# Attention scores of a two-layer decoder trunk with 128-row operands in place of 64-row ones

## The chip, the cores and the metric

The kernel runs on one core of a Trainium2 chip. The metric is the device time of one execution in microseconds. TensorE (PE) does the matrix products and transposes; it has two streams, the loads of the stationary operand (PEld) and the products (PE). VectorE (DVE), ScalarE (ACT) and GpSimd (POOL) do the rest, and SyncE (SP) issues the transfers.

## What is computed

The reference is a trunk of two layers over 256 tokens of width 1024. Each layer is a half-step SwiGLU, a token mixer and a second half-step SwiGLU, each with its own norm, shift, scale and gate. The mixer of layer 0 is forgetting attention, that of layer 1 a dilated window attention with three groups of keys per head. Both have 16 heads of width 64:

```python
# layer 0, per head and block of 128 queries (kv_len = 128 or 256)
logits = einsum("bhqd,bhkd->bhqk", q, k[:, :, :kv_len]) * hd ** -0.5
logits = logits + cum[:, :, q0:kv_len, None] - cum[:, :, None, :kv_len]
p = softmax(where(causal, logits, -inf));  o = p @ v
# layer 1, per head, block of queries and each of 3 (window, dilation) groups
logits = einsum("bqhd,bqkhd->bhqk", qb, kb) * hd ** -0.5
```

In layer 0 the term of the query alone cancels in the softmax, so the kernel adds the key's term only (the bias product below). In layer 1 the three groups share one softmax, since they are merged by their denominators.

## The kernel before

All large products have float32 accuracy out of float32r operands: a weight unit of 512 KiB is loaded by SP (`raw`), split by ACT into a high part `wh` (line 206) and by DVE into a low part `wl` (line 215), and used in three products, high by high, low by high and high by low. The class `Weights` keeps up to five units split ahead of their use. PE's order is written by hand: `tick()` passes once per half unit of weights, and work queued with `at(delay, fn)` is issued after so many ticks, between the weight products. The orders on DVE, ACT and POOL come from a scheduler.

The two mixers go through the heads in four groups of four (`HG`), and for each group:

- `in_proj` makes q and k of the four heads for both token tiles (two banks of [128 tokens, 256 of q | 256 of k]). `head_norm` (line 852) takes the norm of each head: ACT squares, DVE sums, POOL takes the root (lines 858 and 860), DVE scales into `qn`.
- `head_transpose` (line 872) turns `qn` on PE (line 878) into a bank [64 x 2 heads, pair, token]. DVE copies the q half with its gain into `qT` (line 880), ACT the k half into `kT` (line 881). In both, the even head of a pair lies on partitions 0 to 63 and the odd head on 64 to 127.
- For group 0 of the dilated mixer `head_stack` (line 883) does the same in float32r parts: `qs` has a head's high part on its own 64 rows and its low part on the other 64, `ks` the high part of k twice, `kl` the low part of k on the head's own rows.
- `attention` (line 902) runs eight steps per group of heads, one per head and token tile. `scores` puts the logits of a step into a bank; DVE adds the mask and takes the row extremum (line 916), ACT the exponential (line 918). Two or three ticks later `turn` transposes the result on PE (line 928) and ACT copies it to `pt` (line 930). `values` multiplies it with v for two heads at once, in different columns of the array (line 941). `close` and `normalize` divide by the sums.

A step of layer 0 (line 1094 and 1095) is a bias product with all 128 rows over 256 columns, in float32r, and one float32 product of `qT` and `kT` on the head's 64 rows, over 128 columns for token tile 0 and 256 for tile 1. A step of layer 1 is a product `qs` by `ks` with 128 rows (line 1288), `qs` by `kl` on 64 rows (line 1289), and two float32 products on 64 rows, one for each of the groups 1 and 2 (line 1294). PE runs a float32 product as two instructions. There are 32 steps in each mixer.

At the end of each sub-layer `Boundary` (line 414) adds the residual and makes the next input, for token tile 0 and then tile 1; its square root is one small POOL instruction per tile (line 411), DVE's scaling (line 460) waits for it, and PE's transposes (line 469) for that. PE runs products of tile 0 with the next four units meanwhile (`FIRST`).

Of the kernel before, what the change touches and what calls it, by code (L numbers as in the profile page):

```python
# [91 lines left out]
def trunk_kernel(ctx, tc, x_in, c_in, positions, mod_w, mod_b, norm_g, w_gate, w_up, w_down,  # L92
# [43 lines left out]
    def spread_out(delay, steps):  # L136
        """Runs the steps of a generator two ticks after one another."""
# [116 lines left out]
    mods = {}  # L254

    class Mods:
        """The vectors in the order of their use, a k-tile of mod_w at a time."""
# [52 lines left out]
        def finish(self, v, acc):  # L310
# [50 lines left out]
    class Pump:  # L361
        """Spreads the vectors of a phase over its first units."""
# [22 lines left out]
    def mm_blocks(o, k, wh, wl, first, last):  # L385
        """Four blocks of 128 columns of a unit's k-tile against all tokens: o[i // 2][:, i % 2] is [128 columns, S]."""
# [27 lines left out]
    class Boundary:  # L414
        """Residual, norm and transposed input of the next sub-layer for one token tile, in steps."""
# [59 lines left out]
    def two_tiles(n, n_first, products, pump):  # L475
        """Runs products(i, unit, t) over both token tiles for n units, tile 0 leading by n_first units."""
# [112 lines left out]
    def ffn(l, i, s, pool, n_first, new_mods, permute=False, opening=None):  # L589
# [36 lines left out]
        def combine(blk, sg, up):  # L626
            """Two 128-column blocks, transposed already."""
# [43 lines left out]
    def open_trunk(wg, wu, pool):  # L671
        """The first sub-layer's norm and first 512 columns, two k-tiles at a time as the modulation comes in."""
# [43 lines left out]
        def load_mod(q, rows):  # L716
            """Shift and scale columns of group q from the mod_w rows of k-tiles `rows`."""
# [134 lines left out]
    def head_norm(o, pool, then):  # L852
        """RMS norm over each 64-wide head slice of o [P, 512] (PSUM)."""
# [559 lines left out]
```

## Time and profile before

| | |
|---|---|
| time, median of 3 runs (lowest to highest) | 1246.32 us (1245.99 to 1246.4) |
| span of the profiled execution, first to last instruction | 1244.0 us |
| around the span (median less span) | 2.3 us |
| busy: PE, PEld, DVE, ACT, POOL | 1225.0, 1090.4, 935.3, 653.7, 97.1 us |
| mean granted clock of TensorE | 0.999 |
| layer 0's mixer, from its first products to its last | about 216 to 358 us |
| layer 1's mixer | about 747 to 1047 us |

The time of the profiled execution is its span and the part around it that the profile does not cover; the page gives the span, and 2.3 us is taken for what lies around it. The duration of a PE instruction runs from its start to its modelled end and overlaps the next one's, so what a product costs is read from start to start. "64\*128" in a row is rows by columns of the array in use, "128x256" the partitions by elements that are streamed. In the rows, [0.25 <-issue] is idle time of the engine just before the instruction and what ended it.

### The profile page before, as it was taken

How to read it: one execution, taken by the hardware profiler on the slowest of the kernel's cores; microseconds unless marked ns; L12 is line 12 of the kernel's file. 1: busy time of each engine (PE TensorE's matmuls, PEld its weight loads, DVE VectorE, ACT ScalarE, POOL GpSimd, SP SyncE). 2: the span in 40 equal slices, each digit the busy share in tenths (PEclk: the TensorE clock that was granted, in tenths of full speed). 3: DMA queues.
4: the chain of work that ended last, by engine and by line, in shares of the span. 5: the costliest groups of instructions: out<-in, count | busy, mean ns of one | idle time of the engine just before them, and what ended most of it. 6: DMA issues, size and time to landing. Idle time of an engine off the chain costs nothing.

```text
span 1244.0 us, 20956 instructions
## 1 busy us (share of the span) xinstructions
PE 1225.0 (98%) x8130; PEld 1090.4 (88%) x8130; DVE 935.3 (75%) x1318; ACT 653.7 (53%) x978; POOL 97.1 (8%) x120
## 2 busy tenths in 40 slices
PE   6999999999999999999999999999999999999998
PEld 5999988877779999889999888878788787999987
DVE  7879777987778787569988659878686867765653
ACT  4446444665654655444554436566565655544440
POOL 1000000122010000000000003121121200000000
PEclk9999999999999999999999999999999999999999
DMA  9879885785729988638888647756545552867461
GB/s 334 272 265 330 290 327 166 238 278 179 244 92 328 333 270 317 213 117 287 298 282 325 205 151 237 222 168 208 165 153 188 186 170 85 272 204 219 170 208 47
DMA packets 152067, 281.19 MB, mean 226 GB/s; under 512 B 13424, under 2 KB 79504, under 8 KB 151968
## 3 DMA queue, kind: packets, MB, share of 16 engines
q1 hardware_dynamic: 151968, 279.85, 67.3%
q8 instruction: 64, 1.05, 0.3%
q14 instruction: 35, 0.29, 0.1%
HBM read 277.71 MB, written 2.10 MB: 225 GB/s over the span
## 4 chain that ended last, share of the span: by engine, by line
PE 93%; DVE 2%; DMA 2%; issue 1%; ACT 1%; POOL 0%; POOLq 0%; SPq 0%; DVEq 0%; ACTq 0%
PE bank L394 16%; PE bank L396 15%; PE bank L395 15%; PE block_bank L391 13%; PE block_bank L389 12%; PE block_bank L390 12%; PE obank L941 2%; PE bank L928 2%; PE bank L1095 1%; DMA raw<-in_fox_w_in_dram 1%; PE bank L1294 1%; PE bank L878 1%; PE bank L1289 1%; PE bank L770 1%; PE bank L346 1%
## 5 line engine op out<-in xcount | busy, mean ns | idle before, releaser
L215 DVE TENSOR_TENSOR wl<-raw,wh 128x1024 fp32r<-128x1024 f32 (+1 forms) x360 | 435.0, 1216 | 162.4 <-ACT wh L206 159.4
L206 ACT CAST wh<-raw 128x1024 fp32r<-128x1024 f32 (+1 forms) x360 | 374.6, 1046 | 310.4 <-PE bank L396 118.2
L389 PE MATMUL block_bank<-hTh,wh 128*128 128x256 f32 x1312 | 371.9, 283 | 2.0 <-ACT hTh L783 2.0
L391 PE MATMUL block_bank<-hTh,wl 128*128 128x256 f32 x1312 | 371.6, 283 | 0.0
L390 PE MATMUL block_bank<-hTl,wh 128*128 128x256 f32 x1312 | 370.6, 282 | 0.0
L389 PEld LDWEIGHTS block_bank<-hTh,wh 128*128 128x128 f32 x1312 | 248.5, 189 | 2.5 <-ACT hTh L783 2.1
L390 PEld LDWEIGHTS block_bank<-hTl,wh 128*128 128x128 f32 x1312 | 248.2, 189 | 0.5 <-DVE hTl L786 0.2
L391 PEld LDWEIGHTS block_bank<-hTh,wl 128*128 128x128 f32 x1312 | 247.8, 189 | 0.0
L394 PE MATMUL bank<-wh,hTh 128*128 128x512 f32 (+2 forms) x496 | 192.1, 387 | 0.0
L396 PE MATMUL bank<-wh,hTl 128*128 128x512 f32 (+2 forms) x496 | 181.6, 366 | 0.0
L395 PE MATMUL bank<-wl,hTh 128*128 128x512 f32 (+2 forms) x496 | 181.1, 365 | 0.0
L296 DVE SCALAR_TENSOR_TENSOR acc<-mraw,ccols,acc 128x1024 f32<-128x1024 f32 x112 | 143.2, 1279 | 21.2 <-DMA mraw<-in_mod_w_dram 21.0
L395 PE MATMUL bank<-wl,aTh 128*128 128x512 f32 (+1 forms) x420 | 146.4, 349 | 0.0
L394 PE MATMUL bank<-wh,aTh 128*128 128x512 f32 (+1 forms) x420 | 146.1, 348 | 0.0
L396 PE MATMUL bank<-wh,aTl 128*128 128x512 f32 (+1 forms) x420 | 145.7, 347 | 0.0
L394 PEld LDWEIGHTS bank<-wh,hTh 128*128 128x128 f32 x496 | 93.4, 188 | 19.5 <-issue 3.7
L396 PEld LDWEIGHTS bank<-wh,hTl 128*128 128x128 f32 x496 | 93.2, 188 | 16.6 <-DVE hTl L471 0.5
L395 PEld LDWEIGHTS bank<-wl,hTh 128*128 128x128 f32 x496 | 93.6, 189 | 12.1
L394 PEld LDWEIGHTS bank<-wh,aTh 128*128 128x128 f32 x420 | 79.5, 189 | 10.8
L396 PEld LDWEIGHTS bank<-wh,aTl 128*128 128x128 f32 x420 | 79.3, 189 | 10.5
L395 PEld LDWEIGHTS bank<-wl,aTh 128*128 128x128 f32 x420 | 79.5, 189 | 10.1
L918 ACT ACTIVATE lo<-lo,nm 128x128 f32<-128x128 f32 (+1 forms) x64 | 37.9, 592 | 43.2 <-DVE nm L916 43.0
(221 smaller groups left out, 1270.6 us busy)
## 6 DMA issues: line engine op xcount, KB each, us to landing
mraw<-in_mod_w_dram SPq DMA_DIRECT2D x128, 512.0 KB, 5.4
raw<-in_ffn_w_down_dram SPq DMA_DIRECT2D x88, 512.0 KB, 4.4
raw<-in_ffn_w_gate_dram SPq DMA_DIRECT2D x76, 512.0 KB, 4.2
raw<-in_ffn_w_up_dram SPq DMA_DIRECT2D x76, 512.0 KB, 4.1
raw<-in_dil_w_in_dram SPq DMA_DIRECT2D x128, 256.0 KB, 3.8
raw<-in_fox_w_in_dram SPq DMA_DIRECT2D x36, 256.0 KB, 4.4
oraw<-in_mod_w_dram SPq DMA_DIRECT2D x32, 256.0 KB, 6.3
raw<-in_ffn_w_gate_dram SPq DMA_DIRECT2D x24, 256.0 KB, 5.2
```

The lines of the kernel that those rows point to most:

```text
L206: act.copy(wh, self.raws[self.hi])
L215: dve.tensor_sub(wl, self.raws[self.lo], wh.bitcast(F32))
L296: dve.scalar_tensor_tensor(acc, raw, ccol[:, k:k + 1], self.bias_tile if k == 0 else acc, op0=OP.mult, op1=OP.add)
L389: pe.matmul(out_i, wh[:, blk], hTh[:, :, k, :], start=first and i % 2 == 0, stop=False)
L390: pe.matmul(out_i, wh[:, blk], hTl[:, :, k, :], start=False, stop=False)
L391: pe.matmul(out_i, wl[:, blk], hTh[:, :, k, :], start=False, stop=last and i % 2 == 1)
L394: pe.matmul(o, ah, wh, start=first, stop=False)
L395: pe.matmul(o, ah, wl, start=False, stop=False)
L396: pe.matmul(o, al, wh, start=False, stop=last)
L918: act.activation(lo[:, 0:n], lo[:, 0:n], AF.Exp, bias=nm, scale=-1.0, accum_out=sums[:, t, i:i + 1])
L928: pe.transpose(tp[:, b, :], lo[:, b * P:(b + 1) * P], ident)
L941: pe.matmul(ob[0][rows, i // 2, t, :], vb[b], pts[h, t][:, b, :], start=b == 0, stop=b == n - 1)
```

## The change

Every product of the scores gets 128 rows. In layer 0 and for groups 1 and 2 of layer 1, q goes into a tile `qz` with a place per head parity: the head's own 64 rows hold q, the other 64 rows are zero, so that the product with all 128 rows of `kT` (both heads of a pair) gives the head's own logits. For group 0 of layer 1, `kl` gets such a place per parity instead. POOL writes the zeros once per mixer, when its tiles are made (`padded`), and every group of heads uses these tiles again. `head_transpose` now copies k on ACT first, then the q of even heads on ACT and that of odd heads on DVE. The bias product takes 128 columns for token tile 0. `lo` moves to the boundary's tag `u` (three buffers where it had two), `wide` and `on` to its tag `gy`. The sets that only assertions read are left out of the diff, and so are comments.

```diff
+    def padded(pool, shape, dt, name):
+        z = pool.tile([P, 2] + shape, dt, name=name)
+        for e in range(2):
+            rows = z[(1 - e) * HD:(2 - e) * HD, e]
+            nc.gpsimd.memset(rows if dt == F32 else rows.bitcast(F32), 0.0)
+        return z
...
-        dve.tensor_scalar(qT[:, :, tok], tp[:, 0:2, :], gain, None, op0=OP.mult)
         act.copy(kT[:, :, tok], tp[:, 2:4, :])
+        act.activation(qz[0:HD, 0, :, tok], tp[0:HD, 0:2, :], AF.Copy, scale=gain[0:HD])
+        dve.tensor_scalar(qz[HD:P, 1, :, tok], tp[HD:P, 0:2, :], gain[HD:P], None, op0=OP.mult)
...
-            dve.tensor_sub(kl[own, :, tok], k, kh.bitcast(F32))
+            dve.tensor_sub(kl[own, e, :, tok], k, kh.bitcast(F32))
...
-            lo = pool.tile([P, 512], F32, tag="lo", bufs=2, name="lo")
+            lo = main.tile([P, 512], F32, tag="u", bufs=3, name="lo")
...
-            wide = pool.tile([P, NT, HG, HD], F32, tag="on", bufs=2, name="wide")
+            wide = main.tile([P, NT, HG, HD], F32, tag="gy", bufs=2, name="wide")
...
+        qzs = [padded(pool, [2, S], F32, f"qz{b}") for b in range(2)]
...
-                pe.matmul(lg[:, 0:S], idr[:, h:h + 1].to_broadcast([CUM, P]), ncum, start=True, stop=False)
-                pe.matmul(lg[:, 0:n], qT[lo_p:lo_p + HD, pair, t * P:(t + 1) * P],
-                          kT[lo_p:lo_p + HD, pair, 0:n], start=False, stop=True)
+                pe.matmul(lg[:, 0:n], idr[:, h:h + 1].to_broadcast([CUM, P]), ncum[:, 0:n], start=True, stop=False)
+                pe.matmul(lg[:, 0:n], qz[:, i % 2, i // 2, t * P:(t + 1) * P], kT[:, i // 2, 0:n],
+                          start=False, stop=True)
...
                 pe.matmul(lg[:, 0:S], qs[:, e, pair, tok], ks[:, e, pair, :], start=True, stop=False)
-                pe.matmul(lg[:, 0:S], qs[own, e, pair, tok], kl[own, pair, :], start=False, stop=True)
+                pe.matmul(lg[:, 0:S], qs[:, e, pair, tok], kl[:, e, pair, :], start=False, stop=True)
...
-                    pe.matmul(lg[:, c:c + n], qTs[g][lo_p:lo_p + HD, pair, t * P:(t + 1) * P],
-                                     kTs[g][lo_p:lo_p + HD, pair, keys], start=True, stop=True)
+                    pe.matmul(lg[:, c:c + P], qTs[g][:, e, pair, tok], kTs[g][:, pair, tok], start=True, stop=True)
...
+        kl = padded(pool, [2, S], F32R, "kl")
+        qzs = [None] + [padded(pool, [2, S], F32, f"qz{g}") for g in range(1, ND)]
```

PE's order is the same but for the operands. POOL's order gets the zeros. On POOL at the boundary into layer 0's mixer, line 411 is the root of tile 0 and then of tile 1, `fl` a tile of the mixer, and line 858 and 860 the first head norms. Before:

```order
L411 TENSOR_TENSOR rs<-msq,mhalf 128x1
L1048 MEMSET fl 128x256
L411 TENSOR_TENSOR rs<-msq,mhalf 128x1
L858 TENSOR_SCALAR hms<-hms 128x8
L860 TENSOR_TENSOR hrs<-hms,mhalf 128x8
```

One clearing, of `fl`, stands there between the two roots. POOL at the same place now:

```order
L1056 MEMSET fl 128x256
L877 MEMSET qz_2480 64x512 x2
L877 MEMSET qz_2483 64x512 x2
L411 TENSOR_TENSOR rs<-msq,mhalf 128x1
L858 TENSOR_SCALAR hms<-hms 128x8
L860 TENSOR_TENSOR hrs<-hms,mhalf 128x8
```

Four clearings stand ahead of the root of tile 1. At the boundary into layer 1's mixer, where nothing stood between the two roots, there are six now:

```order
L411 TENSOR_TENSOR rs<-msq,mhalf 128x1
L877 MEMSET kl 64x512 x2
L877 MEMSET qz_8314 64x512 x2
L877 MEMSET qz_8317 64x512 x2
L411 TENSOR_TENSOR rs<-msq,mhalf 128x1
```

On ACT in layer 0's mixer, while the third group of heads is turned and the second is scored (lo: exponentials, pt: copies after the transposes), before:

```order
L930 COPY pt<-bank_3263 128x256
L918 ACTIVATE lo,sums<-lo,nm 128x256
L918 ACTIVATE lo,sums<-lo,nm 128x128
L881 COPY kT<-bank_3298 128x2x128
L930 COPY pt<-bank_3287 128x128
L318 CAST wh<-acc 128x1024
L930 COPY pt<-bank_3317 128x256
L918 ACTIVATE lo,sums<-lo,nm 128x256
L881 COPY kT<-bank_3329 128x2x128
```

Each copy of k comes late, since it is second at its bank. ACT at the same place now:

```order
L938 COPY pt<-bank_3270 128x256
L926 ACTIVATE lo,sums<-lo,nm 128x256
L887 COPY kT<-bank_3305 128x2x128
L888 ACTIVATE qz_2480<-bank_3305,fgain 64x2x128
L926 ACTIVATE lo,sums<-lo,nm 128x128
L318 CAST wh<-acc 128x1024
L938 COPY pt<-bank_3294 128x128
L938 COPY pt<-bank_3325 128x256
L887 COPY kT<-bank_3337 128x2x128
L926 ACTIVATE lo,sums<-lo,nm 128x256
L888 ACTIVATE qz_2480<-bank_3337,fgain 64x2x128
```

Each turned tile has one more ACT instruction, and the copies stand nearer to the transposes, ahead of an exponential. On both engines the instruction that reads the turned bank second waits for the first: before, ACT's copy for DVE's; now DVE's copy (line 889) for ACT's two.

## Rows read from the trace of the kernel before

**Rows 1.** The page: busy time of PE, and the chain that ended last by engine.

```profile
PE 1225.0 (98%) x8130; PEld 1090.4 (88%) x8130; DVE 935.3 (75%) x1318; ACT 653.7 (53%) x978; POOL 97.1 (8%) x120
...
PE 93%; DVE 2%; DMA 2%; issue 1%; ACT 1%; POOL 0%; POOLq 0%; SPq 0%; DVEq 0%; ACTq 0%
```

**Rows 2.** Windows of the two mixers: length, then PE, PEld, DVE, ACT, POOL busy, clock, DMA.

```profile
216.00:358.00 142.00, 140.09 (x791) 107.62 (x790) 113.80 (x201) 87.07 (x197) 27.77 (x30) 1.00 0.66 219
...
747.00:1047.00 300.00, 298.80 (x1731) 242.77 (x1730) 233.25 (x398) 184.33 (x314) 54.89 (x49) 1.00 0.57 185
```

**Rows 3.** Timeline of PE, a step of layer 1: start, duration, what.

```profile
801.11 0.28 PE L1288 MATMUL bank<-ks,qs 128*128 128x256 f32 x1
801.32 0.38 PE L1289 MATMUL bank<-kl,qs 64*128 64x256 f32 x1
801.54 0.60 PE L1294 MATMUL bank<-kT,qT 64*128 64x128 f32 x4
802.07 0.50 PE L394 MATMUL bank<-wh,hTh 128*128 128x512 f32 x1
802.41 0.39 PE L395 MATMUL bank<-wl,hTh 128*128 128x512 f32 x1
```

**Rows 4.** Timeline of PE's weight loads in the same step.

```profile
801.31 0.18 PEld L1289 LDWEIGHTS bank<-kl,qs 64*128 64x128 f32 x1 [0.25 <-issue]
```

**Rows 5.** Timeline of PE: six float32 products with 128 rows among float32r products.

```profile
249.85 0.39 PE L396 MATMUL bank<-wh,hTl 128*128 128x512 f32 x1
250.08 0.83 PE L1084 MATMUL bank<-table,fl 128*128 128x128 f32 x6
250.66 0.48 PE L394 MATMUL bank<-wh,hTh 128*128 128x512 f32 x1
250.98 0.39 PE L395 MATMUL bank<-wl,hTh 128*128 128x512 f32 x1
```

**Rows 6.** Timeline of PE: float32r products of 256 columns with 128 rows.

```profile
215.39 0.28 PE L394 MATMUL bank<-wh,aTh 128*128 128x256 f32 x1
215.51 0.28 PE L395 MATMUL bank<-wl,aTh 128*128 128x256 f32 x1
```

**Rows 7.** Timeline of PE, a step of layer 0 for token tile 1.

```profile
254.69 0.28 PE L1094 MATMUL bank<-ncum,idr 128*128 128x256 f32 x1
254.90 0.70 PE L1095 MATMUL bank<-kT,qT 64*128 64x256 f32 x2
255.52 0.50 PE L394 MATMUL bank<-wh,hTh 128*128 128x512 f32 x1
255.86 0.39 PE L395 MATMUL bank<-wl,hTh 128*128 128x512 f32 x1
```

**Rows 8.** Waits: engine and line, whom it waited for: total us, times, longest.

```profile
ACT wh L206 <- PE bank L396: 118.2, 89, 2.1
```

**Rows 9.** Groups of instructions by form: busy us, mean ns, idle before and its releaser.

```profile
L881 ACT COPY kT<-bank 128x256 f32<-128x256 f32 x24 | 8.9, 371 | 5.1 <-DVE qT L880 4.9
L896 ACT ACTIVATE qs<-bank,gain 64x256 fp32r<-64x256 f32 x16 | 7.5, 469 | 1.6 <-DVE kl L899 1.5
L880 DVE TENSOR_SCALAR qT<-bank,gain 128x256 f32<-128x256 f32 x16 | 7.7, 479 | 3.1 <-PE bank L878 3.0
```

**Rows 10.** Timeline of ACT and of PE, the first exponential of layer 1 and its transposes.

```profile
807.11 0.19 ACT L918 ACTIVATION_READ_ACCUMULATOR lo<-lo,nm 128x1 f32 x1
...
807.44 0.60 PE L928 MATMUL bank<-ident,lo 128*128 128x128 f32 x4
```

**Rows 11.** Timeline of POOL: a clearing at the start, and both boundaries into a mixer.

```profile
1.45 0.95 POOL L266 MEMSET bias<- 128x1024 f32 x1
...
216.74 0.31 POOL L1048 MEMSET fl<- 128x256 f32 x1 [3.10 <-PE bank L396]
219.77 0.67 POOL L411 TENSOR_TENSOR rs<-msq,mhalf 128x1 f32<-128x1 f32 x1 [2.71 <-DVE msq L407]
...
747.09 0.60 POOL L411 TENSOR_TENSOR rs<-msq,mhalf 128x1 f32<-128x1 f32 x1 [6.19 <-DVE msq L407]
```

More of the change, by code (lines that the diff above doesn't have):

```diff
@@ L868, in head_norm, with head_transpose @@
         at(HEAD_GAP, scale)
-    turned, keep = set(), []
-    def head_transpose(qn, qT, kT, t, gain):
-        turned.add((id(qT), t))
-        keep.append(qT)
+    turned, holds, keep = set(), {}, []
+    def padded(pool, shape, dt, name):
[4 more added lines that the diff above has]
+        return z
+    def head_transpose(qn, qz, kT, t, gain, g):
+        holds[id(qz), t] = g
         tp = bank4()
@@ L879, in head_transpose, with head_stack @@
         tok = slice(t * P, (t + 1) * P)
-        dve.tensor_scalar(qT[:, :, tok], tp[:, 0:2, :], gain, None, op0=OP.mult)
         act.copy(kT[:, :, tok], tp[:, 2:4, :])
-    def head_stack(qn, qs, ks, kl, t, gain):
-        turned.add((id(qs), t))
+        act.activation(qz[0:HD, 0, :, tok], tp[0:HD, 0:2, :], AF.Copy, scale=gain[0:HD])
+        dve.tensor_scalar(qz[HD:P, 1, :, tok], tp[HD:P, 0:2, :], gain[HD:P], None, op0=OP.mult)
+    def head_stack(qn, qs, ks, kl, t, gain, g):
+        holds[id(qs), t] = g
         keep.append(qs)
@@ L1087, in cumulate, with heads @@
                 dve.tensor_sub(ncum[low, cols], cp[low, :], ncum[low, cols].bitcast(F32))
-        def heads(g, qT, kT):
+        def heads(g, qz, kT):
             def logits(i, t, lg):
-                assert "cum" in turned and all((id(qT), q) in turned for q in range(t + 1))
+                assert "cum" in turned and all(holds[id(qz), q] == g for q in range(t + 1))
                 h = g * HG + i
-                lo_p, pair, n = (i % 2) * HD, i // 2, (t + 1) * P
-                pe.matmul(lg[:, 0:S], idr[:, h:h + 1].to_broadcast([CUM, P]), ncum, start=True, stop=False)
-                pe.matmul(lg[:, 0:n], qT[lo_p:lo_p + HD, pair, t * P:(t + 1) * P],
-                          kT[lo_p:lo_p + HD, pair, 0:n], start=False, stop=True)
+                n = (t + 1) * P
+                pe.matmul(lg[:, 0:n], idr[:, h:h + 1].to_broadcast([CUM, P]), ncum[:, 0:n], start=True, stop=False)
+                pe.matmul(lg[:, 0:n], qz[:, i % 2, i // 2, t * P:(t + 1) * P], kT[:, i // 2, 0:n],
+                          start=False, stop=True)
             return (logits, lambda t: ((t + 1) * P, masks[t]),
@@ L1116, in do_qk @@
             qk = in_proj(2 * GW, 2, pump, n_first if FOX_ORDER[0] == ("qk", g) else 0)
-            qT = pool.tile([P, 2, S], F32, tag="qT", bufs=2, name="qT")
+            qz = qzs[g % 2]
             kT = pool.tile([P, 2, S], F32, tag="kT", bufs=2, name="kT")
@@ L1120, in do_qk @@
                 head_norm(qk[t], pool, lambda qn, t=t: at(
[L1121 to L1122 removed]
+                    NORM_FOX + t - HEAD_GAP, lambda: head_transpose(qn, qz, kT, t, gain, g)))
+            qkT[g] = qz, kT
         def do_heads(g):
@@ L1279, in rope, with heads @@
             dve.tensor_tensor(q4[:, :, :, both], a, b, op=OP.add)
[L1281 removed]
+        def heads(hg, qTs, kTs, vs):
             def logits(i, t, lg):
[L1283 to L1287 removed]
+                assert all(holds[id(q), r] == hg for q in qTs for r in range(NT))
+                e, pair, tok = i % 2, i // 2, slice(t * P, (t + 1) * P)
+                qs, ks = qTs[0], kTs[0]
                 pe.matmul(lg[:, 0:S], qs[:, e, pair, tok], ks[:, e, pair, :], start=True, stop=False)
[L1289 removed]
+                pe.matmul(lg[:, 0:S], qs[:, e, pair, tok], kl[:, e, pair, :], start=False, stop=True)
                 c = S
                 for g in range(1, ND):
[L1292 to L1296 removed]
+                    pe.matmul(lg[:, c:c + P], qTs[g][:, e, pair, tok], kTs[g][:, pair, tok], start=True, stop=True)
+                    c += P
             def vblk(i, t):
@@ L1327, in dilated @@
             attention(hg, LAST_FIRST if last else DIL_FIRST, 1 if last else 2, (T_DIL, PV_DIL),
-                      LAST_PV if last else DIL_PV, *heads(qTs, kTs, vs), oTh, oTl, done, pool, by_tile=last)
+                      LAST_PV if last else DIL_PV, *heads(hg, qTs, kTs, vs), oTh, oTl, done, pool, by_tile=last)
             vp = in_proj(2 * GW, 2, pump)
```

24 lines of the change are left out of this document (6 added, 18 removed).

## The prediction

> **What bounds the kernel now.** I read the page first, then the two mixers by windows, then PE's timeline step by step. The page says that PE is busy for 98% of the span and that 93% of the chain that ended last is PE [rows 1]: what PE saves is saved, as long as nobody else becomes late. The windows say the same of the two stages that the change touches: PE is busy for 140.09 of 142 us and for 298.80 of 300 [rows 2]. But busy is not productive. In a scoring step of layer 1 the products start 0.21, 0.22 and then 0.53 us (for four) after one another, and after the step the first weight product holds the next one up for 0.34 us [rows 3]. The load for the first 64-row product came 0.25 us late and waited for nothing that the profile shows [rows 4], where loads otherwise run ahead. To see what these products cost without that, take three pitches from start to start. A float32r product of 512 columns takes 250.08 - 249.85 = 0.23 us. The six float32 instructions with all 128 rows and 128 columns, and the one float32r product behind them, take 250.98 - 250.08 = 0.90, so (0.90 - 0.23) / 6 = 0.11 each; going into them and out of them costs nothing [rows 5]. A float32r product of 256 columns takes 0.12 [rows 6].
>
> **The term that the change removes.** A layer 1 step takes 802.41 - 801.11 = 1.30 us up to the second weight product behind it [rows 3]. By the pitches it needs 2 x 0.12 (lines 1288 and 1289) + 4 x 0.11 (line 1294) + 0.23 = 0.91. So 0.39 us are lost at two places. Going from 128 rows to 64, the 128-row product is held 0.09 too long and the first 64-row product waits 0.10 for its own load, which is not hidden. Coming back, the four take 0.53 instead of 0.44, and the weight product 0.34 instead of 0.23. With all operands at 128 rows no product of the step changes the shape of the array, so I take the whole 0.39 out: 32 x 0.39 = 12.5 us.
>
> A layer 0 step of tile 1 takes 255.86 - 254.69 = 1.17 us [rows 7]. Its bias product lasts 0.21 instead of 0.12 and the weight product behind 0.34 instead of 0.23, the same two signs. The two instructions of line 1095 take 0.62 together; less the 0.10 and 0.09 found in layer 1 that is 0.215 each, for 256 columns in float32. That a float32 instruction costs the same with 64 and with 128 rows is read at 128 columns: 0.44 / 4 = 0.11 [rows 3] against 0.11 [rows 5]. Without the changes of shape: 0.12 + 2 x 0.215 + 0.23 = 0.78, again 0.39 less. Steps of tile 0 have the same two changes. 32 x 0.39 = 12.5 us.
>
> The bias product of tile 0 goes from 256 columns to 128. No row has a 128-row float32r product of 128 columns. It saves at most half, 16 x 0.06 = 1.0 us, and at least nothing. The nearest row is the float32 instruction of 128 columns at 0.11 [rows 5], so I take 0.01: 16 x 0.01 = 0.2 us. Sum of the gains: **25.2 us**.
>
> A rule speaks against padding. The rows show the 64-row products of a step one after another at 0.11 us each, never two at a time [rows 3]; all products of a step lie on the same head's 64 rows. The Trainium skill, "TensorEngine Tiling (Array Packing)", section "When to Use Tiling", says that a contraction of at most 64 rows should rather use two row tiles, which work independently, up to twice as fast. By the rows padding gives nothing up here and the sum stays 25.2 us; by the rule, if it were already at work, padding would pay for it, and that is a rival below.
>
> **What it adds.** ACT gets one copy per turned tile, 24 of them (8 in layer 0, 16 in layer 1). The nearest row is line 896, also 64 partitions by 256 with a gain: 0.469 us [rows 9]. That is 3.8 us on ACT in layer 0 and 7.5 in layer 1, where it is busy for 87.07 of 142 and 184.33 of 300 us [rows 2]; even in windows shorter by 12.7 and 12.5 us that is covered. DVE's copy keeps its 256 columns, so I leave its 0.479 us [rows 9].
>
> The order at the bank turns round. Before, ACT's copy of k waited for DVE, 4.9 us in all [rows 9]. Now DVE waits for ACT's two copies, 0.37 + 0.47 = 0.84 us if ACT takes them at once. Behind that DVE instruction stand splits, mask steps and modulation sums. 24 x 0.84 = 20 us, of it 6.7 in layer 0 and 13.4 in layer 1: DVE would stand at 113.8 + 6.7 = 120.5 of about 129.3 us and 233.3 + 13.4 = 246.7 of 287.5. It does not become the bound, but in layer 0 it is near. Who waits for it first? Not the weight products: ACT's casts wait 118.2 us in all for PE to free their buffers [rows 8], so the splits run well ahead. It is rather the chain from mask step over exponential to `turn`, whose distance is set in ticks, and ticks get shorter by 0.39 with each step in them. At the first exponential of layer 1 the margin is 807.44 - (807.11 + 0.19) = 0.14 us [rows 10]. Between scores and transposes lie the way out of its own step (0.20) and one whole other step (0.39): 0.59 is taken away, so PE waits 0.45, and with one more ACT copy (0.47) ahead 0.9 us. I count **0.9 us** there, and 0.4 (an estimate, half as much again) for all other steps together; the bounds are nothing, and 0.9 at each of the eight groups of heads, 7.2 us.
>
> POOL clears four tiles of 512 columns ahead of the root of tile 1 at the first boundary, and six at the second. 256 columns took 0.31 and 1024 took 0.95 us, so 512 lie between these; on the line through both it is 0.52 [rows 11]. At the first boundary the memory came free at 216.74 and the root's input at 219.77: 3.03 us, against 0.31 + 4 x 0.52 = 2.4, so nothing is late. At the second boundary, by the same code, 3.0 us lie before 747.09 [rows 11], against 6 x 0.52 = 3.1: **0.1 us** late. PE's transposes wait for that root through DVE's scaling, so it counts in full. At 0.95 each it would be 1.1 + 2.7 = 3.8 us, at 0.31 each nothing. The tiles moved to other tags keep two buffers or get a third; I cost that at nothing, since their other users, the boundaries, lie outside the mixers. No transfer is added or moved.
>
> Sum: 25.2 - 0.9 - 0.4 - 0.1 = 23.8 us. The profiled span of 1244.0 becomes 1220.2, and with the 2.3 us around it **1222.5 us**, against the median of 1246.32.
>
> **The rivals.**
> *The gain is eaten in part by the second reader.* Each of the 24 turned tiles makes a mask step late by more than its margin and costs PE 0.3 to 0.5 us: 7 to 12 us in place of the 1.3 counted, a time of 1228 to 1233. For it speaks how near DVE is to full in layer 0, and the margin of 0.14 us [rows 2, 10]; against it, that ACT's copies now stand sooner after the transposes than its copy of k did, which waited for DVE [rows 9].
> *The change of shape is not what costs.* If the lost time came with the type or the half-empty bank and not with the rows, the steps would stay and the time would be 1246 to 1247. Against it: line 1289 is float32r and pays on 64 rows, and line 1084 is float32 and pays nothing on 128 [rows 3, 5].
> *The 64-row products overlapped.* Then padding pays (4 x 0.11 + 0.12) / 2 = 0.28 us more per step of layer 1 and on the mean (0.11 + 0.215) / 2 = 0.16 per step of layer 0, 14 us in all: 1236. The rule named above would make it so; the starts in rows 3 speak against it.
> *Slower: DVE becomes the bound of the mixers.* It has 142 - 113.8 = 28.2 us free in layer 0 and 66.7 in layer 1 [rows 2]. If ACT, with its casts and exponentials ahead, lets DVE stand for more than 28.2 / 8 = 3.5 us per turned tile in layer 0 and 66.7 / 16 = 4.2 in layer 1, DVE alone fills the old windows; at 5 us it is 24 x 5 = 120 us of waiting for 95 free, 25 us slower than before: 1271. Against it: 0.84 us is what is needed, and ACT's own waits for DVE in the old order were 4.9 us in all [rows 9].
>
> **How the numbers follow.** The forecast has 0.78, the first rival 0.16, the second 0.02, the third 0.01, the slower one 0.03. A measurement of this kernel can tell 0.2%, 2.5 us, from no change. Faster by more: 0.78 + 0.16 + 0.01 = 0.95; within it 0.02; slower 0.03. The range begins where nothing is lost and the bias product halves, 1246.3 - 26.0 = 1220.3, less 0.01 us of rounding on each of the 64 steps, 1219.7, set down to 1219.5. It ends above the forecast with the clearings at their bound (3.7 more, 1226.2), and takes in the near end of the first rival: 1229.
>
> **What would show it.** Right: a layer 1 step takes 0.91 us from its first start to the second weight product, a layer 0 step of tile 1 0.78, no load in a step waits on "issue", and the two mixers last about 130 and 288 us with PE busy throughout, while the products with v (line 941) keep their cost. The root of the second boundary starts 0.1 us later against its input. Wrong: 64 steps that keep 0.2 us or more of the 0.39; PE waiting for exponentials at every group; DVE rows that show long waits on ACT's new copy; or transposes at a boundary that wait 1 us or more for the root.

## The result and the profile after

The changed kernel takes 1230.78 us (median of 4 runs, 1230.07 to 1232.61) against 1246.15 (1245.83 to 1246.4) for the kernel before in the same comparison: ratio 0.988, interval 0.9866 to 0.9894. It is faster by 15.4 us; 23.8 were forecast, and the time lies 1.8 us above the range. The profiled execution took 1230.24 us, with a span of 1228.5.

First the page: busy time of PE, and the chain that ended last by engine.

```profile
PE 1202.4 (98%) x8130; PEld 1085.5 (88%) x8130; DVE 936.6 (76%) x1318; ACT 657.4 (54%) x1002; POOL 101.9 (8%) x130
...
PE 76%; DVE 9%; DMA 5%; issue 4%; POOL 2%; ACT 2%; SPq 0%; POOLq 0%; DVEq 0%; ACTq 0%
```

PE's busy time fell by 22.6 us, near the forecast, but the chain now runs through DVE, DMA and POOL for 16% of the span, where PE alone had 93% [rows 1]. Next the windows of the two mixers, cut at the same products as before.

```profile
215.30:349.30 134.00, 129.20 (x791) 105.74 (x790) 113.52 (x201) 87.68 (x205) 29.30 (x34) 1.00 0.70 232
738.30:1031.60 293.30, 287.44 (x1732) 239.96 (x1731) 234.72 (x398) 186.99 (x330) 55.44 (x50) 1.00 0.59 189
```

They last 134 and 293.3 us where about 130 and 288 were forecast, and PE stands for 4.8 and 5.9 us in them, where it stood for 1.9 and 1.2 [rows 2]. So the steps themselves come next: PE's timeline of the step of [rows 3], and the load that answers to [rows 4].

```profile
792.70 0.28 PE L1295 MATMUL bank<-ks,qs 128*128 128x256 f32 x1
792.81 0.27 PE L1296 MATMUL bank<-kl,qs 128*128 128x256 f32 x1
792.93 0.60 PE L1299 MATMUL bank<-kT,qz 128*128 128x128 f32 x4
793.29 0.48 PE L394 MATMUL bank<-wh,hTh 128*128 128x512 f32 x1
793.61 0.39 PE L395 MATMUL bank<-wl,hTh 128*128 128x512 f32 x1
```

```profile
792.70 0.19 PEld L1296 LDWEIGHTS bank<-kl,qs 128*128 128x128 f32 x1
```

From 792.70 to 793.61 it is 0.91 us, as forecast, and the load starts with the product ahead of it and waits for nothing. The step of layer 0 for token tile 1, in PE's timeline, takes 255.20 - 254.42 = 0.78 us [rows 7]:

```profile
254.42 0.28 PE L1103 MATMUL bank<-ncum,idr 128*128 128x256 f32 x1
254.54 0.59 PE L1104 MATMUL bank<-kT,qz 128*128 128x256 f32 x2
254.78 0.58 PE L394 MATMUL bank<-wh,hTh 128*128 128x512 f32 x1
255.20 0.39 PE L395 MATMUL bank<-wl,hTh 128*128 128x512 f32 x1
```

Both executions have the same 8130 PE products in the same order, so the start of each can be set against the start of the same product before. Over the 64 steps the sum is -24.2 us, -11.7 in layer 0 and -12.4 in layer 1. The term was right; **what failed is what is given back**: outside the steps PE loses 3.7 us in layer 0's mixer and 5.8 in the second boundary and layer 1's mixer, about 9.5 in all, where 1.4 were counted. (The opening, which the change doesn't touch, was 0.7 us shorter in this execution; it differs by as much between executions of one kernel.)

Where are the 9.5 us? PE's waits in layer 1's window name the first place; in the window of before only the wait on `on` stood, with 1.2.

```profile
PE bank L936 <- ACT lo L926: 3.3, 4, 1.6
PE obank L949 <- DVE on L966: 1.7, 1, 1.7
PE bank L469 <- DVE u L460: 0.3, 1, 0.3
PE bank L1295 <- DVE nm L924: 0.3, 1, 0.3
```

The transposes of a step (line 936) wait for its exponential, the exponential for the mask step on DVE (line 924). A slip is the time that a product's start falls behind, set against before, from one product to the next. The largest single slips are 1.48 us at the first exponential of layer 1, 1.74 at 948.7 us, and 1.05 at 309.9 in layer 0. DVE's timeline ahead of the first of them:

```profile
792.82 0.49 DVE L889 TENSOR_SCALAR qz<-bank,gain 64x256 f32<-64x256 f32 x1 [0.43 <-ACT qz L888]
793.34 1.22 DVE L215 TENSOR_TENSOR wl<-raw,wh 128x1024 fp32r<-128x1024 f32 x1
794.60 0.49 DVE L889 TENSOR_SCALAR qz<-bank,gain 64x256 f32<-64x256 f32 x1
795.12 1.28 DVE L296 SCALAR_TENSOR_TENSOR acc<-mraw,ccols,acc 128x1024 f32<-128x1024 f32 x1
796.32 1.22 DVE L215 TENSOR_TENSOR wl<-raw,wh 128x1024 fp32r<-128x1024 f32 x1
797.57 0.69 DVE L924 CUSTOM_DVE_ANT_0 lo<-bank,table 128x512 f32<-128x512 f32 x1
...
940.09 1.28 DVE L296 SCALAR_TENSOR_TENSOR acc<-mraw,ccols,acc 128x1024 f32<-128x1024 f32 x1 [2.78 <-DMA mraw<-in_mod_w_dram]
941.29 0.68 DVE L924 CUSTOM_DVE_ANT_0 lo<-bank,table 128x512 f32<-128x512 f32 x1
...
946.15 0.69 DVE L864 TENSOR_TENSOR qn<-bank,hrs 128x512 f32<-128x512 f32 x1 [2.11 <-POOL hrs L860]
946.87 0.29 DVE L1285 TENSOR_TENSOR ra<-qn,ctab 128x128 f32<-128x128 f32 x1
947.08 0.68 DVE L924 CUSTOM_DVE_ANT_0 lo<-bank,table 128x512 f32<-128x512 f32 x1
```

The scores of that first step began at 792.70. DVE works without a gap from 792.82, and the mask step starts 4.87 us after the scores, behind two copies of q, two splits and a modulation sum (line 296). ACT's exponential follows, behind a table load that ends 0.6 us after the mask step, and then PE [rows 10]:

```profile
797.54 1.28 ACT L926 ACT_TABLE_LOAD   x1
798.83 0.72 ACT L926 ACTIVATE lo<-lo,nm 128x512 f32<-128x512 f32 x1
799.46 0.19 ACT L926 ACTIVATION_READ_ACCUMULATOR lo<-lo,nm 128x1 f32 x1
```

```profile
799.70 0.66 PE L936 MATMUL bank<-ident,lo 128*128 128x128 f32 x4 [1.31 <-ACT lo L926]
```

The 1.48 us can be added up against the same place before. By PE's products alone, transposes that waited for nothing would come 5.52 us after the start of the scores, where they came 6.33 after it before: 0.81 less. The mask step starts 4.87 us after the scores and not 4.29, and from it to the end of the exponential it is 2.08 us and not 1.90. With the margin of 0.14 this makes 0.81 + 0.58 + 0.18 - 0.14 = 1.43 us. The mask step of before, in DVE's timeline, and that of the run with 64-row products below, whose scores began at 800.41:

```profile
805.40 0.68 DVE L916 CUSTOM_DVE_ANT_0 lo<-bank,table 128x512 f32<-128x512 f32 x1
...
805.46 0.69 DVE L924 CUSTOM_DVE_ANT_0 lo<-bank,table 128x512 f32<-128x512 f32 x1
```

At 940 the sum stands 2.78 us for its slice of `mod_w`, with a mask step behind it, and at 946 DVE stands 2.11 us for POOL's root; the transposes of 948.7 wait for the mask step that starts at 947.08. DVE's waits for such slices rose from 21.2 to 29.3 us in all:

```profile
DVE acc L296 <- DMA mraw<-in_mod_w_dram: 29.3, 17, 3.6
```

What the prediction had feared on the engines is small. By forms, DVE's new wait for ACT is 0.7 us in layer 1 (forecast: up to 0.84 at each of 16), and ACT's extra copy costs what was taken [rows 9]:

```profile
L889 DVE TENSOR_SCALAR qz<-bank,gain 64x256 f32<-64x256 f32 x16 | 7.8, 490 | 1.1 <-ACT qz L888 0.7
L888 ACT ACTIVATE qz<-bank,gain 64x256 f32<-64x256 f32 x16 | 7.5, 471 | 0.0
```

And POOL at the second boundary [rows 11]: six clearings in 3.33 us, the root behind them, the slip 0.3 us (0.1 forecast).

```profile
735.32 1.10 POOL L877 MEMSET kl<- 64x512 f32 x2 [3.14 <-PE bank L396]
736.45 2.23 POOL L877 MEMSET qz<- 64x512 f32 x4
738.65 0.64 POOL L411 TENSOR_TENSOR rs<-msq,mhalf 128x1 f32<-128x1 f32 x1
```

### The profile page after: what moved, and what is told of

The parts are those of the page before. It is cut to its first block, busy times and chain, and to the rows that moved or that the text cites. A ratio compares the mean times of both kernels' runs of the same rounds, so it can differ in the third digit from the quotient of the medians.

```text
span 1228.5 us, 21017 instructions
## 1 busy us (share of the span) xinstructions
PE 1202.4 (98%) x8130; PEld 1085.5 (88%) x8130; DVE 936.6 (76%) x1318; ACT 657.4 (54%) x1002; POOL 101.9 (8%) x130
## 3 DMA queue, kind: packets, MB, share of 16 engines
q8 instruction: 64, 1.05, 0.3%
## 4 chain that ended last, share of the span: by engine, by line
PE 76%; DVE 9%; DMA 5%; issue 4%; POOL 2%; ACT 2%; SPq 0%; POOLq 0%; DVEq 0%; ACTq 0%
PE block_bank L389 13%; PE block_bank L391 13%; PE block_bank L390 13%; PE bank L394 11%; PE bank L395 11%; PE bank L396 11%; DMA mraw<-in_mod_w_dram 3%; DVE wl L215 2%; POOL hrs L860 2%; DVE acc L296 1%; DVE lo L924 1%; PE obank L949 1%; DMA raw<-in_dil_w_in_dram 1%; DMA raw<-in_fox_w_in_dram 1%; ACT wh L206 1%
## 5 line engine op out<-in xcount | busy, mean ns | idle before, releaser
L206 ACT CAST wh<-raw 128x1024 fp32r<-128x1024 f32 (+1 forms) x360 | 374.5, 1046 | 299.2 <-PE bank L396 107.2
L296 DVE SCALAR_TENSOR_TENSOR acc<-mraw,ccols,acc 128x1024 f32<-128x1024 f32 x112 | 143.4, 1281 | 29.8 <-DMA mraw<-in_mod_w_dram 29.3
L395 PEld LDWEIGHTS bank<-wl,aTh 128*128 128x128 f32 x420 | 79.5, 189 | 10.1
```

The source lines that it names most:

```text
L206: act.copy(wh, self.raws[self.hi])
L296: dve.scalar_tensor_tensor(acc, raw, ccol[:, k:k + 1], self.bias_tile if k == 0 else acc, op0=OP.mult, op1=OP.add)
L395: pe.matmul(o, ah, wl, start=False, stop=False)
```

## The experiments

Two theories of the 9.5 us. **Theory 1:** the movement of data (ACT's extra copy, the order at the bank, the clearings) delays the chain. **Theory 2:** a step's scores and its transposes lie a fixed number of ticks apart; shorter steps make the ticks shorter, and latency that was covered comes out. All runs in one table. The ratio is to the kernel before, run beside it on the same chip. The last two columns compare the profiled execution with that of before, from the product that began at 216 us to the one at 352 (layer 0's mixer), and from 740 to 1046 (second boundary and layer 1's mixer).

| run | median us | ratio, interval | layer 0 | layer 1 |
|---|---|---|---|---|
| the change | 1230.78 | 0.988 (0.9866 to 0.9894) | -8.0 | -6.7 |
| 64-row products on padded data | 1245.37 | 0.9998 (0.999 to 1.0007) | -0.9 | +0.7 |
| 128-row products, no movement | 1227.17 | 0.9851 (0.9838 to 0.9864) | -8.7 | -10.1 |
| turn one tick later | 1227.77 | 0.9858 (0.9844 to 0.9871) | -8.2 | -10.3 |
| before, turn one tick later | 1246.12 | 1.0004 (0.9994 to 1.0013) | -0.2 | +0.5 |
| DVE writes both halves of q | 1228.14 | 0.9861 (0.9848 to 0.9875) | -9.3 | -8.6 |
| one product writes both halves | 1228.85 | 0.9869 (0.9854 to 0.9884) | -8.3 | -8.7 |
| clearings asked for late | 1228.48 | 0.9868 (0.9854 to 0.9881) | -8.3 | -6.9 |
| no modulation sums | 1223.09 | 0.9814 (0.98 to 0.9829) | -11.5 | -12.2 |
| before, no modulation sums | 1244.76 | 0.9995 (0.9985 to 1.0004) | 0.0 | -0.1 |
| sums that wait for no slice | 1226.47 | 0.9847 (0.9832 to 0.9862) | -7.6 | -11.4 |
| three buffers for slices | 1231.43 | 0.9884 (0.9869 to 0.9899) | -7.8 | -5.2 |
| three slices asked for ahead | 1234.1 | 0.9908 (0.9895 to 0.9922) | -7.2 | -3.6 |
| POOL asks for the slices | 1238.39 | 0.9938 (0.9923 to 0.9953) | -9.2 | -1.0 |
| POOL asks, both edits | 1235.75 | 0.992 (0.9902 to 0.9937) | -8.7 | -3.1 |
| sums on POOL, both edits | 1256.81 | 1.0089 (1.0072 to 1.0107) | -8.9 | +19.9 |
| both edits | 1226.55 | 0.9848 (0.9833 to 0.9862) | -7.3 | -10.6 |
| both edits, warm table | 1231.25 | 0.9883 (0.9867 to 0.99) | -9.0 | -5.7 |
| both edits, later turn in layer 1 alone | 1226.7 | 0.985 (0.9834 to 0.9866) | -10.0 | -11.2 |

How finely can this be read? "Clearings asked for late" turned out to have the change's instructions in the change's order on every engine: POOL's order is a scheduler's, and it put the clearings ahead of the root again. So it is a repeat: 0.3 us apart in the mixers, 2.3 in the medians. The two runs with both edits and with the warm table have one layer 0, and differ by 1.7 us there. Only differences of 2 us or more are read.

**Movement or shape.** The first run puts the changes of shape back on the changed data:

```diff
-  pe.matmul(lg[:, 0:n], qz[:, i % 2, i // 2, ...], kT[:, i // 2, 0:n], ...)
+  pe.matmul(lg[:, 0:n], qz[own, i % 2, i // 2, ...], kT[own, i // 2, 0:n], ...)
```

> The changed kernel with its clearings, its tiles by parity, its third reader at the bank and its short bias product, but with score products that read the head's own 64 rows alone, as before. The changes of shape are back, so the 25 us are not gained. Theory 1 (the movement of data, that is ACT's extra copy, DVE's wait for ACT and the clearings, gives the 9.8 us back): 1246.2 + 9.8 - 0.2 = 1255 to 1257 us. Theory 2 (the movement costs next to nothing while a step lasts as long as before; what is given back is latency that shorter steps no longer cover): 1245.5 to 1247.5 us.

1245.37: all of the movement, with the change's instructions in the change's order on every engine, costs 0.7 us outside the steps, less than can be read, with 0.3 each at the first exponential and at the second boundary. As a cost of its own, theory 1 falls. At that exponential the mask step starts 5.05 us after its scores, and the exponential ends 6.60 after them. The change has 4.87 and 6.95 there, and the kernel before 4.29 and 6.19. Yet the slip is 0.35 in place of 1.48: half of the lateness is there already, and the longer steps cover it. The second run keeps the short steps and drops the movement (`qT`, `kT` and `kl` as before):

```diff
-  pe.matmul(lg[:, 0:n], qz[:, i % 2, i // 2, ...], kT[:, i // 2, 0:n], ...)
+  pe.matmul(lg[:, 0:n], qz[:, i // 2, ...], kT[:, i // 2, 0:n], ...)
```

> The changed kernel with 128-row score products on the queries and keys as before lays them out: no parity tiles, no clearing, no extra ACT copy, and DVE reads the bank first. The scores of the two heads of a pair are so added up in each product, and the output is of such scores. Theory 1: 1246.2 - 24.2 = 1221 to 1223.5 us, and PE's waits for the exponentials fall back to what they were before. Theory 2: the steps are as short as in the changed kernel and the waits stay: 1228 to 1231 us.

1227.17, between the two. Outside the steps 4.8 us are lost, half of the 9.5. Movement alone costs 0.7, short steps alone 4.8, both 9.5: 3 to 4 us come from the two together (by the table's columns this run lost 4.1 us less than the change and 3.6 less than its repeat), on data movement that is harmless while steps are long. Neither theory was whole.

**Distance.**

```diff
-T_FOX = 2
-T_DIL = 3
+T_FOX = 3
+T_DIL = 4
-PV_FOX = 3
+PV_FOX = 2
```

> The changed kernel with one tick more between a step's scores and its transposes in both mixers (T_FOX 3, T_DIL 4), and in layer 0 one tick less from there to the products with v. Theory 2: PE's waits on the exponential (10.4 us in rows of PE and PEld together, which overlap; slips of about 5.5 us) go, the waits on the bias sums, on the bank and on mod_w stay: 1224 to 1227 us. Theory 1 says the same of those waits if only ACT and DVE are late, so this run tells the size of the term, not its origin. If the transposes of a later tick fall behind a wait that only moved on, 1229 to 1231.

> The kernel before with the turn one tick later (T_FOX 3, T_DIL 4, PV_FOX 2), nothing else. If the tick distance covered the latency of mask step and exponential before the change, as the theory of covered latency has it, a later turn gains nothing there: 1245.5 to 1247 us. If such waits stood in the kernel before already: 1242 to 1245.

On the changed kernel 3.6 us come back in layer 1 and nothing in layer 0; on the kernel before the same edit does nothing. That is theory 2's mark: the latency was there and covered. The median alone (1227.77) isn't told from the repeat's; it is the windows that show it, and they do so again in the two other versions that have this distance in layer 1, with q's halves on DVE and nothing more (both edits, -10.6, and the last row of the table, -11.2).

**The copies at the bank.** One run lets DVE write both halves of q, the next does it with one product of 512 columns by a gain with a zero column, without clearings of `qz`:

```diff
-  act.copy(kT[:, :, tok], tp[:, 2:4, :])
-  act.activation(qz[0:HD, 0, :, tok], tp[0:HD, 0:2, :], AF.Copy, scale=gain[0:HD])
+  dve.tensor_scalar(qz[0:HD, 0, :, tok], tp[0:HD, 0:2, :], gain[0:HD], None, op0=OP.mult)
+  act.copy(kT[:, :, tok], tp[:, 2:4, :])
```

> The changed kernel without ACT's extra copy: DVE writes both halves of q, the first without waiting for ACT, and ACT copies k alone, as before. Clearings stay. Theory A (the changed order at the bank, with DVE's wait for ACT and ACT's extra copy, makes up the 3.6 us that the run without movement gained): 1227 to 1228.5 us, ACT's waits for the mask step back near 58. Theory B (any added work on the chain of DVE and ACT costs; here DVE does 24 x 0.49 = 11.8 us more): 1230 to 1233.

```diff
+  dve.tensor_tensor(qz[:, :, :, tok], tp[:, None, 0:2, :].to_broadcast(...), gain2[...].to_broadcast(...), op=OP.mult)
```

> The changed kernel with one DVE instruction in place of the two copies of q: the turned q times a gain of two columns, each zero on the other parity's rows, writes both padded halves at once (512 columns, by the mask step of 512 about 0.68 us in place of 0.49). No extra ACT copy, no wait of DVE for ACT, and only the tile of k's low part is still cleared. Theory A: the time of the run without movement, 1226.5 to 1228. Theory B: DVE's 24 x 0.2 = 5 us more cost something in the steps, 1228.5 to 1230.5.

Both gain 1.7 to 2.0 us in layer 1 against the change and its repeat, although DVE has more to do. That is just below what can be read, and the medians don't tell them from the repeat (1228.48). It may point to ACT's extra copy and the order at the bank as the share that movement has; it doesn't show it, and doesn't part the two. The clearings:

```diff
+CLEAR = 6
+  at(CLEAR, clear)
```

> The changed kernel with the clearings asked for six ticks into the mixer and not at its beginning, so that POOL takes the second token tile's root first. By the trace the root of the second boundary was late by 0.3 us and nothing else waits for the clearings: 1230.3 to 1230.7 us, the slip at 740 us gone, every other slip kept. If the clearings hold more (transposes of the first heads, the first exponential of layer 1): 1228 to 1229.5.

As said, this moved nothing. What a late clearing would bring wasn't tried.

**What stands ahead of the mask step.** One run leaves seven of eight modulation sums of the mixers out; its control does so in the kernel before; a third keeps the sums but lets them read a tile that lies in SBUF:

```diff
+  if k == 0 or v not in MODS_FOX + MODS_DIL:
       dve.scalar_tensor_tensor(acc, raw, ccol[:, k:k + 1], ...)
```

> The changed kernel without the modulation sums of DVE in the two mixers: of each vector summed there only the first of eight slices of mod_w enters (the loads of all slices stay), so that DVE has 42 instructions of 1.28 us less to do and never stands for a slice. If the mask steps are late because DVE's queue holds such sums ahead of them (waiting or not), the waits of PE for exponentials go, the mixers get 7 us or more of the 9.5 lost back: 1220.5 to 1224 us. If the lateness comes from the copies at the bank and from ACT alone: 1226 to 1229.

> The kernel before with the same sums left out as in the run without sums (one of eight slices of each mixer vector enters). If sums cost nothing while the steps are long, since the latency is covered: 1244.5 to 1246.5 us (by the waits of PE in the two mixers, 1.1 us at the most to gain). If DVE's queue costs the kernel before as much as the changed one: 1237 to 1240.

```diff
+  src = self.bias_tile if k and v in MODS_FOX + MODS_DIL else raw
-  dve.scalar_tensor_tensor(acc, raw, ccol[:, k:k + 1], ...)
+  dve.scalar_tensor_tensor(acc, src, ccol[:, k:k + 1], ...)
```

> The changed kernel, but seven of the eight sums of each vector of the two mixers read a tile that already lies in SBUF in place of their slice of mod_w (all slices are still loaded), so that these sums are done at once and DVE has the same work. If it is the waiting for late slices that holds the mask steps up: DVE's waits of 29.3 us fall below 10 and the time goes to that of the run without sums, 1221 to 1224.5 us. If it is the sums' own 1.28 us in the queue: 1227 to 1230.5.

Without sums the mixers lose 1.1 us outside the steps instead of 9.5, with movement, clearings and short steps all in place. In the kernel before, the same sums cost nothing. So the short steps uncover what the sums do on DVE's queue (42 instructions of 1.28 us; whether any other work of that size would do the same was not tried). Whether it is their waiting or their work is less clear. With sums that wait for no slice the median, 1226.47, lies between the two expected ranges; layer 1 loses 1.0 where it lost 5.8, which speaks for the late slices there. But the scheduler gave that run another order on DVE, and its share isn't parted from that of the waiting. Layer 0 loses 4.3. Of this, 1.85 us is one slip that the change doesn't have, at 251.6 us, where in the new order sums stand ahead of the tile `fl` that PE waits for; the slip of 1.05 at 309.9, behind a slice, is gone. For layer 0 the runs leave open which of the two it is. PE's waits in layer 1's window without sums, then with sums that don't wait, then the wait for `fl` in layer 0 of the last:

```profile
PE obank L950 <- DVE on L967: 1.2, 1, 1.2
PE bank L470 <- DVE u L461: 0.3, 1, 0.3
```

```profile
PE obank L950 <- DVE on L967: 1.2, 1, 1.2
PE bank L937 <- ACT lo L927: 0.6, 1, 0.6
PE bank L470 <- DVE u L461: 0.3, 1, 0.3
```

```profile
PE bank L1094 <- DVE fl L1083: 1.7, 1, 1.7
```

**Earlier slices.** A third buffer, with the head norm's squares in another tag to make room; then also a third load at the start, without which no slice is asked for earlier:

```diff
-  raw = rawp.tile([P, D], F32, tag="mraw", bufs=2, name="mraw")
+  raw = rawp.tile([P, D], F32, tag="mraw", bufs=3, name="mraw")
```

> The changed kernel with three buffers in place of two for the slices of mod_w (room for it: the squares of the head norm share the tag gy, the opening's columns move to the opening's pool). Theory 2 in the form that DVE stands for late mod_w slices ahead of mask steps: the 29.3 us of DVE's waits for them fall below 10 and the slips at 310, 935 and 949 us go, 3 us: 1227 to 1228.5. If those slips come from the order on DVE alone: 1230 to 1231.5. Theory 1: 1230 to 1231.5.

> As the run with three buffers for slices of mod_w, but now the third load is asked for at the start too, so that each slice is asked for one step earlier. If late slices hold the mask steps up: DVE's waits for them fall from 29.3 to below 12 us, the slips at 310, 935 and 949 us go, 1227 to 1229 us. If the loads stand in SP's queue behind weight loads that wait, or if the mask steps are late by DVE's own order: waits of 20 us or more, or waits gone and time kept, 1230 to 1231.5.

No gain: with the third buffer alone DVE's waits for slices rose, to 36.9 us; with the third load they fell to 21.5 only, and layer 1 lost 3 us more. The room was made at a price that these runs don't part from the buffer. Then POOL asks for layer 1's slices in SP's place:

```diff
-  nc.sync.dma_start(raw, mod_w[l, k * P:(k + 1) * P, col:col + D])
+  queue = nc.gpsimd if (l, s, j) in MODS_DIL else nc.sync
+  queue.dma_start(raw, mod_w[l, k * P:(k + 1) * P, col:col + D])
```

> The changed kernel, with the slices of mod_w for layer 1's mixer asked for by POOL in place of SP, so that these requests no longer stand behind weight loads that wait for their buffers. If late slices cost layer 1 what the run without that wait showed (4.7 us) and POOL asks in time: DVE's waits for slices in layer 1 fall from 18.6 below 5 us, 1225 to 1228 us. If POOL's own queue (the roots of the head norms, requests that wait for a free buffer) makes slices or roots late, or its requests take longer to land: 1229 to 1236.

> The same with the turn one tick later and q's halves written by DVE. The two edits alone gave 3.95 us in layer 1's mixer; with the slices in time, layer 1 could come to the 5.5 that the run without sums gained there, layer 0 stays: 1224 to 1226 us. If POOL's queue is in the way: 1228 to 1235.

DVE's waits for slices in layer 1 fell from 18.6 to 7.2 us, yet the time rose, with both edits too (1235.75 against 1226.55 without POOL's requests). In the first of the two runs four sums came in a bunch, between 819.73 and 829.65 us. PE's timeline, and the windows ahead of, in and behind the stop:

```profile
830.32 0.79 PE L395 MATMUL bank<-wh,hTh 128*128 128x512 f32 x1 [3.79 <-DVE nm L925]
830.91 0.63 PE L396 MATMUL bank<-wl,hTh 128*128 128x512 f32 x1
831.34 0.63 PE L397 MATMUL bank<-wh,hTl 128*128 128x512 f32 x1
```

```profile
820.00:826.50 6.50, 6.50 (x46) 4.97 (x45) 4.28 (x6) 2.72 (x5) 1.05 (x2) 1.00 0.88 292
826.50:830.30 3.80, 0.03 (x1) 0.00 (x0) 3.58 (x6) 1.53 (x3) 2.30 (x3) 0.96 0.77 226
830.30:834.00 3.70, 3.68 (x12) 2.95 (x13) 2.95 (x4) 3.32 (x7) 3.54 (x4) 0.57 0.57 163
834.00:838.00 4.00, 4.00 (x23) 3.38 (x22) 3.92 (x10) 3.92 (x10) 0.75 (x2) 1.00 0.94 342
```

PE waited 3.79 us for a mask step, ahead of which DVE did two sums (each waiting for its slice) and a reduction within that stop. Against the same products in the change, PE was 0.1 us ahead at 826 us and 5.4 behind at 834: the stop, and the lower clock behind it, are nearly all that layer 1 lost in that run. So earlier slices didn't pay in any of the four runs that tried for them, and what slices in time would bring was not shown by a kernel that does all its sums.

**Sums on POOL**, as a product and an addition, with both edits:

```diff
+  nc.gpsimd.tensor_scalar(raw, raw, ccol[:, k:k + 1], None, op0=OP.mult)
+  nc.gpsimd.tensor_tensor(acc, raw, add_to, op=OP.add)
```

> With the later turn and q's halves on DVE, and the sums of layer 1's mixer as a product and an addition on POOL in place of one instruction of DVE. If POOL does both in 4 us or less and in time, and DVE's other instructions keep their durations: 1224 to 1226 us. If the two engines slow each other down (DVE's splits above their 1.22 us) or the roots of the head norms, which POOL does too, come late behind the sums: 1229 to 1240 us.

The slower branch, and further: 1256.81. By lines in layer 1, POOL needs 3.25 and 2.76 us for what DVE does in 1.28 at once, and DVE's operations on two SBUF tiles get slower. DVE stands 40.5 us for POOL's roots of the head norms, where it stood 13.8 in the change:

```profile
L297 POOL TENSOR_SCALAR mraw<-mraw,ccols 128x1024 f32<-128x1024 f32 x22 | 71.4, 3247 | 67.3 <-DMA mraw<-in_mod_w_dram 67.3
L298 POOL TENSOR_TENSOR acc<-mraw,acc 128x1024 f32<-128x1024 f32 x20 | 55.2, 2758 | 1.7
...
L215 DVE TENSOR_TENSOR wl<-raw,wh 128x1024 fp32r<-128x1024 f32 x79 | 106.9, 1363 | 20.9 <-ACT wh L206 20.1
L868 DVE TENSOR_TENSOR qn<-bank,hrs 128x512 f32<-128x512 f32 x24 | 16.5, 687 | 40.6 <-POOL hrs L864 40.5
L1292 DVE TENSOR_TENSOR qn<-ra,rb 128x128 f32<-128x128 f32 x24 | 16.0, 665 | 0.1
```

**Both edits**, the later turn and q's halves on DVE; then an early exponential of one column; then the later turn in layer 1 alone:

> The changed kernel with both: the turn one tick later and q's two halves written by DVE. By the traces of the two runs alone the mixers gain 0.2 and 3.6 us from the first, 1.25 and 1.9 from the second; where both mend the same wait the larger counts, so 1.2 + 3.6 = 4.8 at least and 7 at most of the 9.5 lost: 1223.5 to 1226 us. If the second edit's longer DVE work undoes the cover of the first: 1227 to 1229.

```diff
+  at(DIL_FIRST - 3, lambda: act.activation(warm, mhalf[:, 0:1], AF.Exp))
```

> As the run with both edits, and a one-column exponential three ticks ahead of the first scores of layer 1, so that ACT's table load of 1.28 us does not stand between its cast and the first exponential. With the later turn the first exponential is in time already, so no more than 0.5 us lower than with both edits: 1223 to 1226 us; the table load moves, nothing else.

> The changed kernel with q's halves written by DVE in both layers and the later turn in layer 1 alone (T_DIL 4), the best setting of each layer so far. Against the kernel before, layer 0's mixer gained 9.3 us with the first edit and layer 1's 10.6 with both, and the tail and lead-in nothing: 1246 - 19.9 = 1225 to 1226.5 us. If layer 1's order on DVE and ACT comes out otherwise with layer 0's shorter distances, 1227 to 1229.

Both edits give 1226.55, between the two expected ranges and 19 us under the kernel before in the same comparison (1245.68). Their interval lies below that of the change and overlaps that of its repeat. The warm table is a miss: PE then waited 2.8 us for ACT's copy of k (line 888), which came late in ACT's new order. The last run has the same ratio as both edits, 0.985; its profiled execution, the fastest of its runs, took 1223.8. Layer 0 shows -10.0 there and -9.3 in the run that has the same layer 0 (DVE writes both halves), against -8.0 and -8.3 in the change and its repeat. What stays open is how a kernel that does all its sums gets the rest: of layer 0's loss nothing came back that can be read.

## Why the prediction was wrong

**The gain.** "I take the whole 0.39 out", 25.2 us with the bias product. Measured 24.2. Steps followed by a weight product gave 0.36 to 0.40. Eight that transposes follow gave 0.34 to 0.35, which is 0.3 us in all. One step holds a wait of 0.5. The shorter bias product was taken at 0.01 us: in the run with 64-row products it gave 0.06 for each step of token tile 0, 0.9 in all, which is near the upper bound of 1.0. In the change these steps gained 0.39 in all, like the others, so if the bias product gave as much there, 0.33 is left for the shape, where 0.39 was taken; the two errors cancel, and that is luck. The two rivals on the shape fall with that: the steps got shorter, and nothing that overlapped was given up, so the rule that spoke against padding was not at work here. The Trainium skill, "TensorEngine Tiling (Array Packing)", section "Key Properties", says that a change of tiling mode drains the engine; the steps agree, with the load in [rows 4] that could not run ahead, and put the price of going to 64 rows and back at 0.39 us in the steps of layer 1 and of token tile 1.

**The loss is the step that failed:** "I count **0.9 us** there, and 0.4 (an estimate, half as much again) for all other steps together". The first exponential cost 1.48; all other places outside the steps, 7.7 without the boundary's 0.3. The mechanism was named (mask step, exponential, turn, with a distance in ticks), but its size was taken from the single margin of [rows 10]. At that place the prediction took "0.59 is taken away" and 0.47 for ACT's copy. The distance shrank by 0.81, since the mask step waits not for the end of its scores but for its turn on DVE, so that both whole steps count. The mask step itself came 0.58 later against its scores. That the bound of 7.2 was reached and passed has two causes. The margin differs from step to step with what stands ahead of the mask step on DVE's queue, and the prediction looked at engine totals there. And the largest thing ahead of it, a modulation sum that may stand for a slice from memory, was in no term: the run without sums got 8.4 of the 9.5 us back, and its control gained nothing from leaving them out. How the 8.4 split into the sums' work and their waiting stays open.

**DVE's wait for ACT**, 20 us if taken whole, was 0.7 in layer 1. The first rival's time (1228 to 1233) was right, but its reason at most in part: where DVE reads first, 1.7 to 2.0 us came back in layer 1, not 7 to 12 in both. That its time held the result is luck. **The clearings** were 0.1 against 0.3; six took 3.33 us, where 3.1 were worked out. **The slower rival** needed DVE to stand for 3.5 us and more per turned tile; its busy time hardly changed (233.25 to 234.72 us in layer 1's windows).

## What to carry to other kernels

A short operation of another array shape among full ones costs at both its ends; padding its operands with zeros can take that out for the price of some copies. But where the order is written in ticks of the work that gets shorter, every distance shrinks with it: list what stands ahead of each consumer on its in-order queue, the instructions that can wait for a transfer first, and set the distances anew with the change.

## What the runs showed of the hardware

- After 3.79 us in which PE stood, the granted clock was 0.57 over the next 3.7 us, with float32r products of 512 columns 0.43 us apart instead of 0.23: mostly the lower of the two levels, 1.2 and 2.4 GHz. From 834 us on it was 1.00 again. In the change itself PE waited 1.7 us at the longest inside the mixers, and the clock stayed at 1.00.
- POOL's sums slow DVE down (the other way round wasn't measured): with them running, DVE's addition of two SBUF tiles of 128 columns (line 1292) went from 285 to 665 ns and the split (line 215) from 1219 to 1363, while the product out of PSUM (line 868) kept 687. The Trainium skill, "GPSIMD Engine Reference", section "Specifications", has POOL share its SBUF interfaces with DVE, with contention where a DVE instruction has two SBUF inputs; the rows agree.
- Some versions with short steps scatter more: the kernel before spread over 0.6 us in four runs beside the change and 1.8 at the most in its other comparisons, the change over 2.5 and (its repeat) 3.0 in two sets of four, the last version over 4.6. Others don't: 0.8 with sums that wait for no slice, 1.0 with the warm table. Why was not tried.
